# A hybrid decoder layer: SSD inputs taken from PSUM, additions moved from GpSimd, attention steps three apart

## The chip, the cores and the metric

The kernel runs on one core of one Trainium2 chip. The metric is device microseconds of one execution, the median of several. Its engines are TensorE (PE, with its weight loads as PEld), VectorE (DVE), ScalarE (ACT), GpSimd (POOL) and SyncE (SP), which issues the DMAs. Each engine works through its own queue in order; semaphores connect them.

## What is computed

One layer (DEPTH = 1) on 512 tokens of width 1024, in float32:

```python
h = rmsnorm(x, norm_mix);  u = h @ w_in          # columns: q k v | z xbc dt | p
y_attn = moba_attention(q, k, v)                  # 6 heads x 64, causal, blocks of 256
y_ssd  = ssd_mixer(xbc, z, dt_raw, ...)           # 6 heads x 64, state 128, chunks of 128
y_pool = pool_mixer(p_in, pool_w, pool_scale)     # trailing means over 2, 4, 8, 16 tokens
x = x + concat([y_attn, y_ssd, y_pool]) @ w_out
h = rmsnorm(x, norm_ffn); gate, up = split(h @ w_gate_up)
x = x + (silu(gate) * up) @ w_down                # hidden width 2816
out = rmsnorm(x, norm_final)
```

In the SSD mixer `xdt = x_h * dt`, `y = y_diag + y_off + x_h * d_skip`, then `y * silu(z)` and a norm over each group of 192 channels. With at most two blocks of 256, the block selection of the attention keeps every earlier block, so it is plain causal attention here.

## The kernel before

Products that need float32 accuracy are split: every operand becomes a rounded part and a remainder (`hi`, `lo`), and `mm3` (L165) multiplies three times, hi by hi, hi by lo, lo by hi. ACT writes the rounded part and DVE (at times POOL) subtracts it for the remainder; so each 128x1024 tile of weights costs an ACT copy and a DVE subtraction (`split`, L136).

The main line of the program writes out the projections one after the other: v, then q and k of the first two heads, the four tiles of B and C, z with dt, q and k again, the three tiles of x, q and k, and the two pooling tiles. Beside it run lanes (`Lanes`, L58): generators for attention, SSD, the transposes of x and B, and pooling. Each `mm3` advances a clock by an estimate of its time (`tick`), and a lane goes on when the clock has passed the time it asked for, or when results that it names are marked as due (`mark(name, after)` puts the due time `after` units ahead; `when` and `ensure` test it). That gives the order in which the program is written; the framework then sets the order on each engine when the kernel is built, by a simulated timeline of its own (L1245), so an engine's order need not be the written one.

The parts that the change touches:

- Attention (`attention_lane`, L635) has 24 steps, one per head and 128 queries. A step's `scores` (L585) multiplies q by k, takes the row minimum with the causal mask on DVE, the exponential and its sum on ACT, the reciprocal (L599) and the scaling of the probabilities (L600) on DVE. Two steps later (`ATT_LAG`) `probs_t` transposes the probabilities on PE (L608), and two steps after that `values` multiplies them by v. The tiles of 512 columns come from a ring of eight (`w2k`), others of 384 from a ring of six (`w384`, `NW`).
- SSD. `xs_lane` (L476) transposes a convolved tile of x on PE and ACT copies it from PSUM to `xs_nat` (L482). `ssd_decay` (L415), per chunk, builds the decay matrices; its mask addition (L424) is on DVE. POOL then makes `xdt` (L431), `xw` (L434) and `sk`, which is x times d_skip (L436). `ssd_products` (L439) does the matmuls, carries the state `prev` from chunk to chunk in two halves (L455 to L458), and sums `y`: `yo` on DVE, its addition into `sk` on POOL (L468), the diagonal part on DVE (L469), the gate `sz` on POOL (L470), the squares on ACT. After the last chunk come the norm and its scalings (L528), transposes (L533) and `mix_out`.
- Pooling. `evac_p` (L669) takes a tile out of PSUM as `pin` (L674), forms window sums by shifted additions on POOL (L677), two for the first tile and four for the second, and ends with `dm` on DVE (L691 to L693); `pool_lane` multiplies `dm` on PE (L700) and scales the product (`mix_out`, L301).
- The output projection's first half (`po`, L740) takes the eight tiles of the mixers' results in the order of `MIX_ORDER`: attention tile 0, pooling tile 0, attention 1, pooling 1, the three SSD tiles, attention 2. The second half and the FFN follow.

Of the kernel before, what the change touches and what calls it, by code (L numbers as in the profile page):

```python
# [26 lines left out]
P = 128  # L27
S = 512
# [14 lines left out]
ATT = (1.2, 0.4, 0.4)  # L43
ATT_LAG = 2
VAL_LAG = 2
SSD = (3.0, 3.0, 1.5)
LAST = 256
NDEC = 4
NW = 6
ENG = ("vvvvv", "vvvvv")  # L50
# [47 lines left out]
def layer(tc, xT, xn, w1, wz, wv, wo, wgu, wd, par, poolw, gffn, gfin, out):  # L98
# [3 lines left out]
    with ctx:  # L102
# [106 lines left out]

        warm = mp.tile([P, S], BF16, name="warm")  # L210
        nc.vector.memset(warm, 0.0)
# [132 lines left out]
        def evac_z(t, ps):  # L344
            nc.vector.scalar_tensor_tensor(dtr[:, t], ps[:, 384:390], rstd[:, t : t + 1], par_sb[:, C_DTB : C_DTB + NH], ALU.mult, ALU.add)
            th = w384(f"thz{t}")
            nc.scalar.activation(th, ps[:, :384], AF.Tanh, scale=hrstd[:, t : t + 1])
            nc.vector.tensor_scalar_mul(sz[:, t], ps[:, :384], hrstd[:, t : t + 1])
            nc.vector.scalar_tensor_tensor(sz[:, t], th, 1.0, sz[:, t], ALU.add, ALU.mult)
            if t == NT - 1:  # L350
                softplus()
                mark("dt", 13.0)

# [18 lines left out]
        bc_sb = [mp.tile([P, S], F32, name=f"bc{i}") for i in range(4)]  # L372
        xs_nat = mp.tile([P, NT, 384], F32, name="xs_nat")
        b_nat = mp.tile([P, 2, NT, P], F32, name="b_nat")
# [22 lines left out]
        ssq = mp.tile([P, 2 * NT], F32, name="ssq")  # L397
        prev = [None, None]
        skip_bc = par_sb[:, C_DSK : C_DSK + NH].unsqueeze(2).to_broadcast([P, NH, 64])
        st1 = {}  # L400
# [14 lines left out]
        def ssd_decay(c):  # L415
# [12 lines left out]
            for g in range(2):  # L428
                nc.vector.tensor_tensor(l3(es[g]), l3(es[g]), ps_g[:, None, g * P : (g + 1) * P].to_broadcast([P, 3, P]), ALU.mult)
            xdt = w384(f"xdt{c}")  # L430
            nc.gpsimd.tensor_tensor(h3(xdt), h3(xs_nat[:, c]), bcast_h(dt_, c), ALU.mult)  # L431
            xw = w384(f"xw{c}")
            if c < NT - 1:
                nc.gpsimd.tensor_tensor(h3(xw), h3(xdt), bcast_h(dte, c), ALU.mult)  # L434
            sk = w384(f"sk{c}")
            nc.gpsimd.tensor_tensor(h3(sk), h3(xs_nat[:, c]), skip_bc, ALU.mult)  # L436
            st1[c] = (es, xdt, xw, sk)

        def ssd_products(c):  # L439
            es, xdt, xw, sk = st1.pop(c)  # L440
            cs = slice(c * P, (c + 1) * P)
            if c < NT - 1:
                ps_s = bank(f"ps_s{c}")
                for g in range(2):
                    nc.tensor.matmul(ps_s[:, g * 192 : (g + 1) * 192], b_nat[:, g, c], xw[:, g * 192 : (g + 1) * 192], start=True, stop=True)
            if c > 0:
                ps_o = bank(f"ps_o{c}")
                for g in range(2):
                    nc.tensor.matmul(ps_o[:, g * 192 : (g + 1) * 192], bc_sb[2 + g][:, cs], prev[g], start=True, stop=True)
            if c < NT - 1:  # L450
                for g in range(2):
                    new = wk.tile([P, 192], F32, name=f"prev{c}{g}", tag=f"prev{g}")
                    src = ps_s[:, g * 192 : (g + 1) * 192]
                    if c == 0:
                        nc.vector.tensor_copy(new, src)  # L455
                    else:
                        nc.gpsimd.tensor_tensor(h3(new), h3(prev[g]), bcast_h(cd, c, 3, 3 * g), ALU.mult)
                        nc.vector.tensor_tensor(new, new, src, ALU.add)  # L458
                    prev[g] = new
            ps_y = bank(f"ps_y{c}")  # L460
            for h in range(NH):
                hs = slice(h * 64, (h + 1) * 64)
                nc.tensor.matmul(ps_y[:, hs], es[h // 3][:, (h % 3) * P : (h % 3 + 1) * P], xdt[:, hs], start=True, stop=True)
            L.clock += 2.6
            if c > 0:
                t_ = w384(f"yo{c}")
                nc.vector.tensor_tensor(h3(t_), h3(ps_o[:, :384]), bcast_h(ea, c), ALU.mult)
                nc.gpsimd.tensor_tensor(sk, sk, t_, ALU.add)  # L468
            nc.vector.tensor_tensor(sk, ps_y[:, :384], sk, ALU.add)  # L469
            nc.gpsimd.tensor_tensor(yz[c], sk, yz[c], ALU.mult)  # L470
            junk = w384(f"jy{c}")
            for g in range(2):
                gs = slice(g * 192, (g + 1) * 192)
                nc.scalar.activation(junk[:, gs], yz[c][:, gs], AF.Square, accum_out=ssq[:, 2 * c + g : 2 * c + g + 1])
# [18 lines left out]
        def ssd_lane():  # L493
# [20 lines left out]
            for c in range(NT):  # L514
# [6 lines left out]
                yield SSD[2]  # L521
            yield 3.0
            nc.vector.tensor_scalar(ssq, ssq, 1.0 / 192, EPS, ALU.mult, ALU.add)
            r = rsqrt(ssq, 2 * NT, "rs2")
            for c in range(NT):
                for g in range(2):
                    gs = slice(g * 192, (g + 1) * 192)
                    nc.vector.tensor_scalar_mul(yz[c][:, gs], yz[c][:, gs], r[:, 2 * c + g : 2 * c + g + 1])  # L528
            yield 7.0
            for m in range(3):  # L530
# [40 lines left out]
        def evac_k(j):  # L571
            def f(ps):
                k = w2k(f"k{j}")
                nc.vector.tensor_tensor(k, ps, rstd_bc, ALU.mult)
                for name, kl, own, other in (("ka", kl_sb[0], H0, H1), ("kb", kl_sb[1], H1, H0)):
# [93 lines left out]
        def evac_p(j):  # L669
            def f(ps):  # L670
# [581 lines left out]
```

## Time and profile before

| | |
|---|---|
| median of 3 runs (lowest to highest) | 577.88 us (576.05 to 577.88) |
| the profiled execution | 577.72 us, its span 576.0 us |
| busy in the span | PE 557.9, PEld 501.6, DVE 463.0, ACT 281.0, POOL 60.1 us |
| granted TensorE clock, mean | 0.990 |

PE busy includes its pipeline: a matmul's recorded time runs on past the start of the next. An instruction's time is from its start to its end; idle time in front of it is put down to the engine whose signal came last.

### The profile page before, as it was taken

To read this page: it belongs to the slowest core of one execution; us is meant where nothing else is said; L and a number is where in the kernel's file an instruction comes from. 1 tells how busy PE (TensorE), PEld (TensorE's weight loads), DVE (VectorE), ACT (ScalarE), POOL (GpSimd) and SP (SyncE) were. 2 spreads that over 40 slices of the span, in tenths; PEclk is the share of its full clock that TensorE was granted. 3 is DMA by queue.
4 is the path that set the end of the run, shared out by engine and by line. 5 is a ranking of instruction groups with operands and counts; after the bars stand their busy time and mean duration, and the time that the engine had idled before them with its cause. 6 is when DMAs were issued, how large, how long until landed. Compare 5 with 4: busy or idle time off the path is not lost.

```text
span 576.0 us, 9083 instructions
## 1 busy us (share of the span) xinstructions
PE 557.9 (97%) x3492; PEld 501.6 (87%) x3492; DVE 463.0 (80%) x838; ACT 281.0 (49%) x481; POOL 60.1 (10%) x75
## 2 busy tenths in 40 slices
PE   7999999999998997999999999999999999999994
PEld 4998998888776886998899989998899889899984
DVE  4387966899989768999899968897689877798445
ACT  5686554667646546464345522643155324325234
POOL 6011002006860000000000000000000000000033
PEclk8999999999999998999999999999999999999998
DMA  7862233422122701245324321443034233222003
GB/s 238 296 209 75 74 109 110 129 75 86 43 75 73 292 0 38 74 126 175 138 75 147 115 106 47 156 128 110 0 121 162 85 109 110 75 73 75 1 0 146
DMA packets 19519, 61.62 MB, mean 107 GB/s; under 512 B 2300, under 2 KB 3476, under 8 KB 19476
## 3 DMA queue, kind: packets, MB, share of 16 engines
q1 hardware_dynamic: 19476, 61.05, 31.6%
q8 instruction: 27, 0.44, 0.3%
q14 instruction: 16, 0.13, 0.1%
HBM read 58.93 MB, written 2.11 MB: 106 GB/s over the span
## 4 chain that ended last, share of the span: by engine, by line
PE 61%; DVE 7%; ACT 1%; issue 1%; DVEq 0%; ACTq 0%
PE psf L166 12%; PE psf L168 11%; PE psf L167 11%; PE pd L166 6%; PE pd L167 6%; PE pd L168 6%; PE po L166 2%; PE po L167 2%; PE po L168 2%; PE ps_h L939 1%; DVE sl L810 1%; DVE E L1059 1%; DVE x L1169 0%; DVE sz L528 0%; ACT sqf L1172 0%
## 5 line engine op out<-in xcount | busy, mean ns | idle before, releaser
L167 PE MATMUL pd<-dl,aTh 128*128 128x512 f32 x160 | 63.3, 395 | 0.0
L166 PE MATMUL pd<-dh,aTh 128*128 128x512 f32 x160 | 62.8, 396 | 0.0
L168 PE MATMUL pd<-dh,aTl 128*128 128x512 f32 x160 | 60.8, 395 | 0.0
L1059 DVE TENSOR_TENSOR E<-psf,E 128x256 f32<-128x256 f32 x110 | 42.4, 418 | 11.2 <-PE psf L168 10.3
L166 PE MATMUL psf<-h_hi,gh 128*128 128x256 f32 x176 | 49.9, 285 | 0.1
L167 PE MATMUL psf<-h_lo,sh 128*128 128x256 f32 x176 | 49.7, 282 | 0.0
L167 PE MATMUL psf<-h_lo,gh 128*128 128x256 f32 x176 | 49.7, 283 | 0.0
L168 PE MATMUL psf<-h_hi,gl 128*128 128x256 f32 x176 | 49.6, 282 | 0.0
L168 PE MATMUL psf<-h_hi,sl 128*128 128x256 f32 x176 | 49.5, 281 | 0.0
L166 PE MATMUL psf<-h_hi,sh 128*128 128x256 f32 x176 | 49.5, 281 | 0.0
L138 DVE TENSOR_TENSOR wlo<-raw,whi 128x1024 fp32r<-128x1024 f32 (+3 forms) x29 | 33.6, 1159 | 18.0 <-ACT whi L137 17.9
L1151 POOL TENSOR_TENSOR x<-x,gf 128x512 f32<-128x512 f32 x4 | 5.1, 1294 | 359.5 <-ACT sqf L774 359.5
L137 ACT ACTIVATE whi<-raw 128x1024 fp32r<-128x1024 f32 (+3 forms) x34 | 31.6, 931 | 22.0 <-PE pc L167 10.0
L166 PE MATMUL pc<-hT_hi,whi 128*128 128x512 f32 x104 | 41.3, 397 | 0.0
L809 ACT ACTIVATE sh<-sb 128x1024 fp32r<-128x1024 f32 x22 | 23.2, 1056 | 36.3 <-PE pd L167 29.8
L168 PE MATMUL pc<-hT_hi,wlo 128*128 128x512 f32 x104 | 40.9, 393 | 0.0
L167 PE MATMUL pc<-hT_lo,whi 128*128 128x512 f32 x104 | 40.8, 392 | 0.0
L766 DVE TENSOR_TENSOR x<-pd,x 128x512 f32<-128x512 f32 x44 | 28.4, 686 | 14.9 <-PE pd L168 14.8
L809 ACT ACTIVATE dh<-r_d 128x1024 fp32r<-128x1024 f32 x22 | 23.1, 1057 | 33.9 <-PE psf L167 22.6
L168 PEld LDWEIGHTS pd<-dh,aTl 128*128 128x128 f32 x160 | 30.1, 188 | 7.3
L166 PEld LDWEIGHTS pd<-dh,aTh 128*128 128x128 f32 x160 | 30.1, 188 | 7.0
L167 PEld LDWEIGHTS pd<-dl,aTh 128*128 128x128 f32 x160 | 30.1, 188 | 6.9
(291 smaller groups left out, 1714.3 us busy)
## 6 DMA issues: line engine op xcount, KB each, us to landing
r_g<-wgu SPq DMA_DIRECT2D x22, 512.0 KB, 3.7
r_u<-wgu SPq DMA_DIRECT2D x22, 512.0 KB, 3.9
r_d<-wd SPq DMA_DIRECT2D x22, 512.0 KB, 3.2
raw<-w SPq DMA_DIRECT2D x13, 512.0 KB, 3.5
raw<-wo SPq DMA_DIRECT2D x8, 512.0 KB, 3.2
rawx<-xT SPq DMA_DIRECT2D x8, 256.0 KB, 3.8
rawn<-xn SPq DMA_DIRECT2D x4, 512.0 KB, 5.1
x<-xn SPq DMA_DIRECT2D x4, 512.0 KB, 7.2
```

What stands on the lines that cost most here:

```text
L137: nc.scalar.activation(hi[:, sl], raw[:, sl], AF.Copy)
L138: eng.tensor_tensor(lo[:, sl], raw[:, sl], hi[:, sl].bitcast(F32), ALU.subtract)
L166: nc.tensor.matmul(ps, s_hi, m_hi, start=first, stop=False)
L167: nc.tensor.matmul(ps, s_hi, m_lo, start=False, stop=False)
L168: nc.tensor.matmul(ps, s_lo, m_hi, start=False, stop=last)
L766: nc.vector.tensor_tensor(x1[t][:, cs], ps, x1[t][:, cs], ALU.add)
L809: nc.scalar.activation(hi, src, AF.Copy)
L810: eng.tensor_tensor(lo, src, hi.bitcast(F32), ALU.subtract)
L939: nc.tensor.transpose(pst[:, j * P : (j + 1) * P], xh[:, kt * P : (kt + 1) * P], ident)
L1059: nc.vector.tensor_tensor(o_, a_, b_, ALU.add)
L1151: nc.gpsimd.tensor_tensor(x1[t][:, :512], x1[t][:, :512], gf[0][:, :512], ALU.mult)
```

## The change

`x*dt` and `x*d_skip` are made directly from the transposes in PSUM, for all four chunks of a tile at once: `xdt` by one DVE product, `skp` by two scaled ACT copies per tile. The lane that does it now also waits for `dt`. `xs_nat` and the per-chunk POOL products go. The additions of `yo` and the six shifted additions of pooling move from POOL to DVE. The state is one tile of 384 columns instead of two of 192; its first copy is on ACT. The probabilities of the third and fourth 128 queries of each head are scaled on ACT instead of DVE. Attention's transposes come three steps after the scores. Due times change for k (5 to 7), pooling (10 to 16) and the x tiles (1 to 2.5), the 384-column ring has three buffers, the warm-up tile lies in `xdt`'s memory, and the squares are written into `sk`.

```diff
-ATT_LAG = 2
+ATT_LAG = 3
-NW = 6
+NW = 3
+E_KL = "g"
+E_SH = "vvvvvv"
+E_YO = "v"
+E_SZ = "g"
+E_PREV = "g"
+E_PR = "vvaa"
+E_RS = "v"
+E_XW = "g"
+M_K = 7.0
+M_DM = 16.0
+M_DT = 13.0
...
+        eng = {"v": nc.vector, "g": nc.gpsimd}
...
-        warm = mp.tile([P, S], BF16, name="warm")
+        xdt = mp.tile([P, NT, 384], F32, name="xdt")
+        warm = xdt[:, 0, : S // 2].bitcast(BF16)
...
-            xdt = w384(f"xdt{c}")
-            nc.gpsimd.tensor_tensor(h3(xdt), h3(xs_nat[:, c]), bcast_h(dt_, c), ALU.mult)
-            xw = w384(f"xw{c}")
+            xw = None
             if c < NT - 1:
-                nc.gpsimd.tensor_tensor(h3(xw), h3(xdt), bcast_h(dte, c), ALU.mult)
-            sk = w384(f"sk{c}")
-            nc.gpsimd.tensor_tensor(h3(sk), h3(xs_nat[:, c]), skip_bc, ALU.mult)
-            st1[c] = (es, xdt, xw, sk)
+                xw = w384(f"xw{c}")
+                eng[E_XW].tensor_tensor(h3(xw), h3(xdt[:, c]), bcast_h(dte, c), ALU.mult)
+            st1[c] = (es, xw)
...
+            sk = skp[:, c]
...
             if c < NT - 1:
-                for g in range(2):
-                    new = wk.tile([P, 192], F32, name=f"prev{c}{g}", tag=f"prev{g}")
-                    src = ps_s[:, g * 192 : (g + 1) * 192]
-                    if c == 0:
-                        nc.vector.tensor_copy(new, src)
-                    else:
-                        nc.gpsimd.tensor_tensor(h3(new), h3(prev[g]), bcast_h(cd, c, 3, 3 * g), ALU.mult)
-                        nc.vector.tensor_tensor(new, new, src, ALU.add)
-                    prev[g] = new
+                new = wk.tile([P, 384], F32, name=f"prev{c}", tag="prev")
+                if c == 0:
+                    nc.scalar.copy(new, ps_s[:, :384])
+                else:
+                    eng[E_PREV].tensor_tensor(h3(new), h3(prev[0]), bcast_h(cd, c), ALU.mult)
+                    nc.vector.tensor_tensor(new, ps_s[:, :384], new, ALU.add)
+                prev[0] = new
...
-                nc.gpsimd.tensor_tensor(sk, sk, t_, ALU.add)
+                eng[E_YO].tensor_tensor(sk, sk, t_, ALU.add)
             nc.vector.tensor_tensor(sk, ps_y[:, :384], sk, ALU.add)
-            nc.gpsimd.tensor_tensor(yz[c], sk, yz[c], ALU.mult)
-            junk = w384(f"jy{c}")
+            eng[E_SZ].tensor_tensor(yz[c], sk, yz[c], ALU.mult)
...
         def xs_lane(m, xs):
-            yield when(f"conv{m}")
+            yield when(f"conv{m}", "dt")
...
-            nc.scalar.copy(xs_nat[:, :, m * P : (m + 1) * P], psx.rearrange("p (c n) -> p c n", c=NT))
-            mark(f"xs{m}", 1.0)
+            src = psx.rearrange("p (c h d) -> p c h d", c=NT, h=2)
+            dst = lambda t_: t_[:, :, m * P : (m + 1) * P].rearrange("p c (h d) -> p c h d", h=2)
+            dt_bc = dt_[:, :, 2 * m : 2 * m + 2].unsqueeze(3).to_broadcast([P, NT, 2, 64])
+            nc.vector.tensor_tensor(dst(xdt), src, dt_bc, ALU.mult)
+            for h in range(2):
+                c0 = C_DSK + 2 * m + h
+                nc.scalar.activation(dst(skp)[:, :, h], src[:, :, h], AF.Copy, scale=par_col(c0))
+            mark(f"xs{m}", 2.5)
...
-                mark(f"k{j}", 5.0)
+                mark(f"k{j}", M_K)
...
-            nc.vector.tensor_scalar_mul(pr[:, :n], pr[:, :n], sm)
+            if E_PR[i] == "v":
+                nc.vector.tensor_scalar_mul(pr[:, :n], pr[:, :n], sm)
+            else:
+                nc.scalar.activation(pr[:, :n], pr[:, :n], AF.Copy, scale=sm)
...
-                def shift_add(dst, src, n, p0=0):
-                    nc.gpsimd.tensor_tensor(dst[p0:, 16:], src[p0:, 16:], src[p0:, 16 - n : 16 - n + S], ALU.add)
+                def shift_add(e, dst, src, n, p0=0):
+                    eng[E_SH[e]].tensor_tensor(dst[p0:, 16:], src[p0:, 16:], src[p0:, 16 - n : 16 - n + S], ALU.add)
...
-                mark(f"dm{j}", 10.0)
+                mark(f"dm{j}", M_DM)
```

## Rows read from the trace of the kernel before

**Rows 1.** Page, busy us (share) and instructions of each engine.

```profile
PE 557.9 (97%) x3492; PEld 501.6 (87%) x3492; DVE 463.0 (80%) x838; ACT 281.0 (49%) x481; POOL 60.1 (10%) x75
```

**Rows 2.** Stretches: length; busy PE, PEld, DVE, ACT, POOL; clock, DMA, GB/s.

```profile
30.00:130.00 100.00, 100.00 (x525) 87.65 (x524) 82.39 (x181) 62.46 (x124) 7.12 (x11) 1.00 0.34 108
130.00:187.00 57.00, 53.69 (x311) 44.98 (x310) 52.55 (x122) 35.06 (x85) 32.22 (x36) 1.00 0.21 69
...
176.30:213.50 37.20, 37.05 (x180) 30.98 (x181) 28.98 (x64) 20.53 (x38) 1.30 (x1) 1.00 0.38 142
```

**Rows 3.** Waits of weight loads, 130:187: us, times, longest.

```profile
PEld po L166 <- ACT mixT_hi L301: 1.8, 1, 1.8
PEld ps_t L608 <- DVE mn L597: 1.4, 2, 1.1
PEld ps_t L608 <- DVE sk L469: 0.8, 1, 0.8
PEld po L166 <- DVE yo L467: 0.8, 1, 0.8
PEld ps_pool L700 <- DVE y L629: 0.7, 1, 0.7
```

**Rows 4.** Timeline at 154.5: start, us, engine, line [idle before <-releaser].

```profile
154.53 1.31 POOL L470 TENSOR_TENSOR sz<-sk,sz 128x384 f32<-128x384 f32 x1 [1.05 <-DVE sm L599]
...
154.90 0.97 DVE L693 TENSOR_TENSOR dm<-dm,pin 128x16 f32<-128x16 f32 x1
```

**Rows 5.** Timeline, 162 to 177 us.

```profile
162.01 0.69 DVE L674 TENSOR_TENSOR pin<-pc,rstd_bc 128x512 f32<-128x512 f32 x1
...
171.35 0.17 DVE L693 TENSOR_TENSOR dm<-dm,pin 128x16 f32<-128x16 f32 x1
171.38 1.03 POOL L468 TENSOR_TENSOR sk<-sk,yo 128x384 f32<-128x384 f32 x1 [1.88 <-DVE dm L692]
...
171.74 0.88 DVE L600 TENSOR_SCALAR pr<-pr,sm 128x384 f32<-128x384 f32 x1
...
173.42 1.05 PE L700 MATMUL ps_pool<-dm,pw 128*128 128x512 f32 x2
...
175.62 0.67 ACT L301 ACTIVATE mixT_hi<-ps_pool,par_sb 128x512 fp32r<-128x512 f32 x1
...
176.34 0.50 PE L166 MATMUL po<-whi,mixT_hi 128*128 128x512 f32 x1 [1.54 <-ACT mixT_hi L301]
```

**Rows 6.** POOL, 130:187: lines (busy, mean ns); busy us of L677.

```profile
L436 POOL TENSOR_TENSOR sk<-xs_nat,par_sb 128x384 f32<-128x384 f32 x4 | 4.8, 1195 | 0.0
...
L468 POOL TENSOR_TENSOR sk<-sk,yo 128x384 f32<-128x384 f32 x3 | 4.0, 1320 | 4.7 <-DVE yo L467 2.8 <-DVE dm L692 1.9
L431 POOL TENSOR_TENSOR xdt<-xs_nat,dt__221 128x384 f32<-128x384 f32 x4 | 3.8, 941 | 15.1 <-ACT xs_nat L482 15.1
...
130.00:187.00 57.00, 7.65 (x6) 1.00 0.21 69
```

**Rows 7.** DVE, L600: 130:187 by shape; busy us in 30:130.

```profile
L600 DVE TENSOR_SCALAR pr<-pr,sm 128x384 f32<-128x384 f32 x3 | 2.2, 742 | 0.1
...
L600 DVE TENSOR_SCALAR pr<-pr,sm 128x512 f32<-128x512 f32 x3 | 1.9, 638 | 0.0
...
30.00:130.00 100.00, 4.74 (x14) 1.00 0.34 108
```

**Rows 8.** DVE, L424: 40:130, then 130:187.

```profile
L424 DVE TENSOR_TENSOR dec<-dec,mask_s 128x384 f32<-128x384 f32 x4 | 2.0, 552 | 0.7 <-DMA dec<-acum_d 0.7
...
L424 DVE TENSOR_TENSOR dec<-dec,mask_s 128x384 f32<-128x384 f32 x4 | 3.1, 780 | 0.2 <-DMA dec<-acum_d 0.2
```

**Rows 9.** Timeline of DVE at 178 us.

```profile
178.82 1.93 DVE L528 TENSOR_SCALAR sz<-sz,rs_y 128x192 f32<-128x192 f32 x8
```

**Rows 10.** Timeline: an exponential's sum and its reciprocal.

```profile
154.68 0.19 ACT L598 ACTIVATION_READ_ACCUMULATOR pr<-pr,mn 128x1 f32 x1
...
156.63 0.16 DVE L599 RECIPROCAL sm<-sm 128x1 f32<-128x1 f32 x1
```

More of the change, by code (lines that the diff above doesn't have):

```diff
@@ L48 @@
 NDEC = 4
-NW = 6
+NW = 3
[10 more added lines that the diff above has]
+M_DT = 13.0
+D_SN = (3.0, 7.0)
 ENG = ("vvvvv", "vvvvv")
@@ L351, in evac_z @@
                 softplus()
-                mark("dt", 13.0)
+                mark("dt", M_DT)
         def softplus():
@@ L372, in layer @@
         bc_sb = [mp.tile([P, S], F32, name=f"bc{i}") for i in range(4)]
-        xs_nat = mp.tile([P, NT, 384], F32, name="xs_nat")
+        skp = mp.tile([P, NT, 384], F32, name="skp")
         b_nat = mp.tile([P, 2, NT, P], F32, name="b_nat")
@@ L397, in layer @@
         ssq = mp.tile([P, 2 * NT], F32, name="ssq")
-        prev = [None, None]
-        skip_bc = par_sb[:, C_DSK : C_DSK + NH].unsqueeze(2).to_broadcast([P, NH, 64])
+        prev = [None]
         st1 = {}
@@ L448, in ssd_products @@
                 for g in range(2):
-                    nc.tensor.matmul(ps_o[:, g * 192 : (g + 1) * 192], bc_sb[2 + g][:, cs], prev[g], start=True, stop=True)
+                    nc.tensor.matmul(ps_o[:, g * 192 : (g + 1) * 192], bc_sb[2 + g][:, cs], prev[0][:, g * 192 : (g + 1) * 192], start=True, stop=True)
             if c < NT - 1:
-                for g in range(2):
-                    new = wk.tile([P, 192], F32, name=f"prev{c}{g}", tag=f"prev{g}")
-                    src = ps_s[:, g * 192 : (g + 1) * 192]
-                    if c == 0:
-                        nc.vector.tensor_copy(new, src)
-                    else:
-                        nc.gpsimd.tensor_tensor(h3(new), h3(prev[g]), bcast_h(cd, c, 3, 3 * g), ALU.mult)
-                        nc.vector.tensor_tensor(new, new, src, ALU.add)
-                    prev[g] = new
+                new = wk.tile([P, 384], F32, name=f"prev{c}", tag="prev")
[5 more added lines that the diff above has]
+                prev[0] = new
             ps_y = bank(f"ps_y{c}")
@@ L462, in ssd_products @@
                 hs = slice(h * 64, (h + 1) * 64)
-                nc.tensor.matmul(ps_y[:, hs], es[h // 3][:, (h % 3) * P : (h % 3 + 1) * P], xdt[:, hs], start=True, stop=True)
+                nc.tensor.matmul(ps_y[:, hs], es[h // 3][:, (h % 3) * P : (h % 3 + 1) * P], xdt[:, c, hs], start=True, stop=True)
             L.clock += 2.6
@@ L521, in ssd_lane @@
                 yield SSD[2]
-            yield 3.0
+            yield D_SN[0]
             nc.vector.tensor_scalar(ssq, ssq, 1.0 / 192, EPS, ALU.mult, ALU.add)
@@ L527, in ssd_lane @@
                     gs = slice(g * 192, (g + 1) * 192)
-                    nc.vector.tensor_scalar_mul(yz[c][:, gs], yz[c][:, gs], r[:, 2 * c + g : 2 * c + g + 1])
-            yield 7.0
+                    r_ = r[:, 2 * c + g : 2 * c + g + 1]
+                    if E_RS == "v":
+                        nc.vector.tensor_scalar_mul(yz[c][:, gs], yz[c][:, gs], r_)
+                    else:
+                        nc.scalar.activation(yz[c][:, gs], yz[c][:, gs], AF.Copy, scale=r_)
+            yield D_SN[1]
             for m in range(3):
@@ L580, in f @@
                     nc.scalar.activation(t_[other], k[own], AF.Copy)
-                    nc.gpsimd.tensor_tensor(kl[own], k[own], t_[own].bitcast(F32), ALU.subtract)
-                mark(f"k{j}", 5.0)
+                    eng[E_KL].tensor_tensor(kl[own], k[own], t_[own].bitcast(F32), ALU.subtract)
+                mark(f"k{j}", M_K)
             return f
@@ L599, in scores @@
             nc.vector.reciprocal(sm, sm)
-            nc.vector.tensor_scalar_mul(pr[:, :n], pr[:, :n], sm)
+            if E_PR[i] == "v":
+                nc.vector.tensor_scalar_mul(pr[:, :n], pr[:, :n], sm)
+            else:
+                nc.scalar.activation(pr[:, :n], pr[:, :n], AF.Copy, scale=sm)
             return pr
@@ L674, in f @@
                 nc.vector.tensor_tensor(pt[:, 16:], ps, rstd_bc, ALU.mult)
-                def shift_add(dst, src, n, p0=0):
-                    nc.gpsimd.tensor_tensor(dst[p0:, 16:], src[p0:, 16:], src[p0:, 16 - n : 16 - n + S], ALU.add)
-                shift_add(wa_, pt, 1)
+                def shift_add(e, dst, src, n, p0=0):
+                    eng[E_SH[e]].tensor_tensor(dst[p0:, 16:], src[p0:, 16:], src[p0:, 16 - n : 16 - n + S], ALU.add)
+                shift_add(3 * j, wa_, pt, 1)
                 if j == 0:
-                    shift_add(wb_, wa_, 2, 64)
+                    shift_add(1, wb_, wa_, 2, 64)
                     nc.scalar.copy(wb_[:64, 16:], wa_[:64, 16:])
                 else:
-                    shift_add(wb_, wa_, 2)
-                    shift_add(wa_, wb_, 4)
-                    shift_add(wb_, wa_, 8, 64)
+                    shift_add(4, wb_, wa_, 2)
+                    shift_add(5, wa_, wb_, 4)
+                    shift_add(2, wb_, wa_, 8, 64)
                     nc.scalar.copy(wb_[:64, 16:], wa_[:64, 16:])
```

4 lines of the change are left out of this document (2 added, 2 removed).

## The prediction

> **What bounds the kernel now.** I read the page first: TensorE (PE) is busy for 557.9 of 576.0 us [rows 1], so whatever this change does on the other engines is worth only what PE waits for them. The busy times by stretch say where that is [rows 2]. From 30 to 130 us PE never stops. From 130 to 187 us, where the tail of the attention, the SSD products, the pooling and the first half of the output projection meet, it is busy for 53.7 of 57.0 us and VectorE (DVE) for 52.6: DVE is nearly full there, and PE waits for it. From 176.3 to 213.5 us PE is full again (37.1 of 37.2). Every instruction that the diff edits runs before 187 us, so the ceiling is what PE loses between 130 and 187 us: at least the 3.3 us that its busy time leaves, at most the 5.5 us that its weight loads waited at five places [rows 3]. I take about 5.
>
> The five places: 1.8 us for the second pooling tile's scaled copy on ScalarE (ACT), 1.4 and 0.8 for DVE in front of transposes of probabilities, 0.8 in front of an output projection, 0.7 for `y` in front of the first pooling matmul. I followed them back in the timeline. At 154.53 us GpSimd (POOL) starts `sz`, which ends at 155.84; a DVE subtraction of 16 columns that starts at 154.90 takes 0.97 us and ends at 155.87 [rows 4], where the same line took 0.17 us at 171.35 [rows 5]. `y` stands behind it. At 171.38 POOL adds `yo` into `sk`, and the DVE scaling at 171.74 takes 0.88 us [rows 5]; with POOL nearly idle that line's mean over all widths is 0.34 us (4.74 over 14) [rows 7]. The 1.8 us end a long chain: the second pooling tile leaves PSUM at 162.01, four additions run on POOL, DVE ends it at 171.52, PE multiplies at 173.42, and ACT delivers at 176.29, 0.05 us before PE starts [rows 5]. So POOL is in most of them, as a link of the chain or by DVE being held.
>
> **The change, part by part, for 130 to 187 us.**
>
> *POOL.* It loses `x*dt` (3.8), `x*d_skip` (4.8), the additions of `yo` (4.0) and the six shifted additions (7.65): 20.2 of its 32.2 us [rows 2, 6]. The state's decay becomes one instruction per chunk instead of two.
>
> *DVE, what comes.* Four shifted additions of 512 columns and two on part of the partitions, at the 0.69 us of a 512-column two-operand pass [rows 5]: 4.1. Three additions of `yo` at the 0.55 us of a 384-column pass in quiet [rows 8]: 1.7. Three products `x*dt` from PSUM at 0.69, of which I count one here, since two of the three convolutions end earlier, where PE has no waits: 0.7. Sum 6.5.
>
> *DVE, what goes.* The six widest probability scalings of this stretch: 2.2 + 1.9 [rows 7]. The state's first copy goes to ACT and two half-width additions become one: two passes near 0.35, 0.7. Sum 4.8.
>
> *DVE, what gets shorter.* In this stretch the mask addition takes 0.78 us against 0.55 in quiet [rows 8], the 384-wide scaling 0.74 against the 0.34 of rows 7. So the four scalings that stay could lose 0.4 each, four mask additions 0.23, the 16-column line 0.8; for the rest (splits, `qa`, `qb`, `dm`), which have no row here, I put 1.5: 4.8 if POOL were silent. With 20.2 of 32.2 gone I take 3.1. The new additions read two operands from SBUF as the mask addition does, so they meet what is left on POOL: from 9 x 0.23 x 0.37 = 0.8, if they fare as the mask additions did beside a POOL 57% busy, to 9 x 0.80 = 7.2, if each is held as the 16-column line was. I take 0.8, as the mask additions are the likest. Net for DVE: 6.5 - 4.8 - 3.1 + 0.8 = -0.6 us. DVE is hardly relieved; what goes is POOL from the chains.
>
> For this the Trainium skill, "SBUF — State Buffer", section "Who interferes with whom", has a rule: a VectorE instruction with two SBUF inputs, or in a two-port mode, and a GpSimd instruction that reads SBUF shut each other out for the whole instruction. By that rule, the trace agrees: the two ends at 155.84 and 155.87. It speaks against the change too, which puts nine such instructions where DVE is fullest; it is the mechanism of the third rival below.
>
> *The waits of PE.* First pooling matmul: 0.7 goes. Transposes behind held scalings: 0.4 and 0.5 of their 1.4 and 0.8. The projection in front of which 0.8 was waited reads the first pooling tile, whose chain shortens: 0.5. The second pooling tile: 9.5 us from PSUM to `dm` become 0.69 + 4 x 0.69 + about 1.1 = 4.6 plus queueing, so 1.6 of 1.8 goes. Sum 3.7. What is late next is the SSD tail, whose normalisation ends on DVE at 180.75 [rows 9]. If PE arrives 3.7 us sooner, that tail must follow. It loses a POOL pass of 1.03 and 0.5 of being held [rows 5], and starts about 1.2 sooner because PE's own products do: 2.7. PE then waits 1.0 us there. Gain 3.7 - 1.0 = 2.7, with a tenth for short waits elsewhere 2.8.
>
> *ScalarE.* It gets the 12 scalings, six of them here, at most 0.67 us each as in the scaled copy of 512 columns [rows 5]: 4.0 us, and six half-width scaled copies instead of three whole ones, about 1 us more. It is busy for 35.1 of 57.0 us [rows 2], which hides the work. A new wait comes: the scaling waits for DVE's reciprocal, and everything behind it on ACT (splits of weights, copies for the next projections, exponentials) waits too, and PE for those. On one step the exponential's sum was out at 154.87 and the reciprocal ran at 156.63 [rows 10]: 1.8 us. The bounds are 0 and 6 x 1.8 = 10.8 us of ACT, against 17 us idle after the additions; I take none on the path and keep the upper end as a rival.
>
> *Order.* Attention three steps apart gives each exponential one more step before PE transposes it, and keeps one more 512-column tile of a ring of eight alive; the `mark` times of the keys (5 to 7) and of pooling (10 to 16) only shift where PE's instructions are written out. Bounds: 2.9 us less (the three waits that are not a pooling tile's) to 1.8 more (one more wait as long as the longest) [rows 3]; I take nothing beside the sum above, which has part of it. The smaller ring (NW 6 to 3) goes with three fewer kinds of tile in it, and the transposes of x wait for `dt`, which is written out a projection earlier: nothing. No DMA is added, and those that SP issues keep their places.
>
> **Sum.** 577.72 us (the profiled execution: span 576.0 and 1.7 around it) - 2.8 = 574.9 us. The median of the runs shown is 577.88, practically the same. A difference under 0.3% (1.7 us) can't be told from none.
>
> **Rivals.**
>
> *The late order eats the gain.* The pooling matmul is written out at 16 clock units instead of 10; if PE's order keeps it where it was, the shorter pooling chain is not used, and of 3.7 only the 1.6 us of the held scalings and `y` go, less the 1.0 at the SSD tail: 577.1. For it: the two pooling waits are 2.1 of the 3.7. Against: the order on PE need not be the written one.
>
> *ACT stands in its own way: slower.* Place: a scaling that waits for the reciprocal, in front of the scaled copy on which PE already waited 1.8 us [rows 3]. Price: 1.8 + 0.67 = 2.5 us there, with the other gains lost: 580.2. It decides once the reciprocal is late by 1.5 us or more in DVE's queue at one of the two pooling tiles. For it: DVE stays 91% full. Against: ACT is idle for 22 of the 57 us.
>
> *Additions held by POOL.* Nine held for 0.80 us: DVE +5.8 instead of -0.6, where 4.4 us of it are idle; the 1.4 us over go to PE and no wait is saved: 579.1. Against it stand the mask additions.
>
> *More than forecast.* All 5 us of PE's loss go, the SSD tail following: 572.7.
>
> **How the numbers follow.** Forecast 0.46, late order 0.24, ACT 0.14, held additions 0.06, more 0.10. The forecast's own range is 573.3 to 576.6, and some nine tenths of it lie over 0.3%: 0.41; with the last case and the lower edge of the late order 0.54 faster. Most of the ACT case, under half of the held additions and a little of the late order are 0.17 slower; 0.29 stay within. For 8 in 10 the range takes the forecast and the late order, most of the larger gain and of the other two: 572.0 to 580.0.
>
> **What the changed profile would show.** POOL's busy time between 130 and 187 us near 12 us; no 16-column line of 0.97 us; scalings that stay on DVE near 0.35 us; from `pin` to the finished `dm` under 7 us; PE's weight loads waiting under 3 us there, most of it for the SSD tail; the stretch after 213 us unchanged, 2 to 3 us earlier. It is wrong if ACT idles before its scalings with PE waiting for a copy behind them, if a shifted addition takes over 1 us, or if the gain or loss lies after 190 us.

## The result, and the profile after

| | before | after |
|---|---|---|
| median of six runs, us | 577.88 (576.05 to 579.16) | 573.43 (570.86 to 573.94) |
| profiled execution, us (span) | 577.72 (576.0) | 570.86 (569.1) |
| mean granted clock of that execution | 0.990 | 0.996 |

The ratio of the times is 0.9917, with an interval from 0.9897 to 0.9937: 4.8 us less, 3.6 to 6.0. Forecast was 2.8 us less.

The two spans lie 6.9 us apart, and two parts of that aren't the change's. The first is the start. In the next fence and the one behind it (stretches; columns as in [rows 2]), PE's clock was granted at 0.72 on average between 6 and 12 us before, and at 1.00 after. The main line's products of the first q and k come first (from 7.1 us before, 5.9 after); the projection of v (`pn`), which follows them, begins at 20.0 us before and at 18.1 us after: 1.9 us. That early the diff touches nothing but the memory of the warm-up tile, and the runs don't show that as the reason: the other kernels with the old tile begin the projection of v at 18.3 to 19.8 us, those with the new one at 18.1 to 19.7. The second is a stretch at half clock among the first products of the FFN, which of this pair only the execution before has. It is read under "half clock" below and is worth 0.85 us. The runs of both kernels fall into groups by mean clock, and like with like (spans 571.7 to 572.2 against 575.5 to 577.5 at 0.988 to 0.991, or 569.1 and 569.2 against some 574.5 at 0.994 to 0.996) the difference is 4 to 5 us, as the ratio has it.

```profile
6.00:12.00 6.00, 4.89 (x13) 3.67 (x14) 4.05 (x4) 4.51 (x7) 3.77 (x4) 0.72 0.89 301
...
224.00:227.00 3.00, 0.36 (x2) 0.37 (x3) 3.00 (x6) 0.23 (x1) 0.00 (x0) 0.94 0.00 0
227.00:230.00 3.00, 3.00 (x16) 2.99 (x15) 1.98 (x4) 1.44 (x3) 0.00 (x0) 0.50 0.49 158
```

The kernel after, its stretches (the second answers to [rows 2]):

```profile
6.00:12.00 6.00, 5.42 (x22) 3.83 (x23) 3.82 (x4) 4.50 (x7) 4.47 (x4) 1.00 0.89 302
...
130.00:187.00 57.00, 56.16 (x325) 48.16 (x324) 52.51 (x126) 37.33 (x88) 11.13 (x16) 1.00 0.32 109
...
218.00:221.00 3.00, 0.38 (x3) 0.38 (x4) 3.00 (x6) 0.21 (x1) 0.00 (x0) 1.00 0.00 0
221.00:224.00 3.00, 2.90 (x26) 2.69 (x25) 2.80 (x6) 1.91 (x4) 0.00 (x0) 1.00 0.43 161
```

Between 130 and 187 us POOL fell from 32.22 to 11.13 us, DVE stayed where it was (52.55 and 52.51), and PE's idle time fell from 3.3 to 0.84 us. What its weight loads still wait for there (answers to [rows 3]):

```profile
PEld ps_t L630 <- ACT pr L622: 0.9, 1, 0.9
PEld po L179 <- DVE skp L478: 0.7, 1, 0.7
PEld ps_o L460 <- issue: 0.6, 1, 0.6
PEld ps_t L630 <- issue: 0.5, 2, 0.3
```

The waits for a pooling tile's copy (1.8) and for DVE ahead of transposes of probabilities (1.4 and 0.8) are gone; no new one stands at the SSD tail. First and last starts of two tiles' matmuls, before and then after (min, median and max ns, first and last start in us), show where the time was won:

```profile
L166 PE MATMUL po<-whi,mixT_hi x64: 387/389/497, 158.9 to 215.6; 128*128 128x512 f32 x64
...
L166 PE MATMUL psf<-h_hi,gh x176: 277/280/561, 219.3 to 538.3; 128*128 128x256 f32 x176
```

```profile
L179 PE MATMUL po<-whi,mixT_hi x64: 387/389/501, 151.8 to 209.6; 128*128 128x512 f32 x64
...
L179 PE MATMUL psf<-h_hi,gh x176: 277/280/385, 213.3 to 531.4; 128*128 128x256 f32 x176
```

With the 1.9 us of the start taken off, the output projection ends 4.1 us sooner, and the FFN begins 4.1 us sooner.

For every kernel below I added up what PE lost: each interval between the starts of two neighbouring matmuls, less the steady interval of their form (0.227 us for 512 columns), and what a half clock adds counts too. Three sums: "early" runs from the projection of v (`pn`) to the last projection of the mixers (`pc`), "tail" from there to the last transpose of the SSD result (`ps_sn`), "later" from there to the first down projection of the FFN. The times are the ratios against the runs of before beside them on the same chip, turned into microseconds of 577.5. "Half" counts the stretches at the lower clock level between 30 and 560 us of the profiled execution. The sums depend on the steady interval that is taken for each form; differences between kernels hold to some 0.4 us.

| kernel | ratio (95%) | us | early | tail | later | half |
|---|---|---|---|---|---|---|
| before | 1 | 0 | 2.9 | 6.2 | 7.0 | 1 |
| after | 0.9917 (0.9897-0.9937) | -4.8 | 2.4 | 2.5 | 6.1 | 0 |
| b1_adds_pool | 0.9930 (0.9911-0.9949) | -4.0 | 2.4 | 3.4 | 6.1 | 0 |
| b2_lag2 | 0.9968 (0.9954-0.9981) | -1.8 | 2.4 | 5.3 | 7.1 | 1 |
| b3_scal_dve | 0.9992 (0.9979-1.0005) | -0.5 | 3.0 | 6.2 | 7.2 | 1 |
| b5_xs_pool | 1.0031 (1.0017-1.0046) | +1.8 | 2.5 | 7.0 | 9.3 | 2 |
| b4_due | 1.0043 (1.0029-1.0058) | +2.5 | 6.1 | 5.2 | 7.2 | 1 |
| c_mk5 | 1.0031 (1.0016-1.0047) | +1.8 | 6.2 | 4.5 | 7.4 | 1 |
| c_mk9 | 0.9965 (0.9951-0.9979) | -2.0 | 3.3 | 3.6 | 7.2 | 0 |
| a1_adds | 1.0047 (1.0029-1.0064) | +2.7 | 3.4 | 7.1 | 8.9 | 1 |
| a2_lag3 | 1.0114 (1.0082-1.0146) | +6.6 | 4.8 | 12.1 | 6.3 | 2 |
| a3_xs | 0.9994 (0.9980-1.0008) | -0.3 | 5.0 | 4.7 | 6.4 | 0 |
| d_before_due | 1.0006 (0.9990-1.0022) | +0.3 | 2.5 | 6.1 | 7.2 | 1 |
| d_before_duelag3 | 0.9998 (0.9986-1.0011) | -0.1 | 2.4 | 6.6 | 7.3 | 2 |

One execution of a2_lag3 (3117 us) and one of d_before_duelag3 (1938 us) are left out of the ratios. Of the 4.95 us that the profiled pair differ by from the projection of v on, some 3.7 lie in the tail, 0.5 before it and 0.85 after it (each rounded).

### The profile page after: what moved, and what is told of

Read it like the earlier page. It is cut to its first block, busy times and chain, and to the rows that moved or that the text cites. A ratio compares the mean times of both kernels' runs of the same rounds, so it can differ in the third digit from the quotient of the medians.

```text
span 569.1 us, 9071 instructions
## 1 busy us (share of the span) xinstructions
PE 553.4 (97%) x3492; PEld 498.8 (88%) x3492; DVE 459.6 (81%) x834; ACT 288.8 (51%) x497; POOL 40.8 (7%) x56
## 4 chain that ended last, share of the span: by engine, by line
PE 85%; DVE 10%; ACT 2%; issue 1%; DMA 1%; SPq 0%; DVEq 0%; ACTq 0%
PE psf L179 12%; PE psf L181 12%; PE psf L180 12%; PE pd L180 7%; PE pd L179 7%; PE pd L181 6%; PE pc L179 4%; PE pc L180 4%; PE pc L181 4%; PE po L179 2%; PE po L180 2%; PE po L181 2%; PE pn L180 2%; PE pn L179 2%; PE pn L181 2%
## 5 line engine op out<-in xcount | busy, mean ns | idle before, releaser
L832 DVE TENSOR_TENSOR sl<-sb,sh 128x1024 fp32r<-128x1024 f32 x22 | 26.8, 1220 | 9.3 <-ACT sh L831 5.5
```

The costliest lines, as they stand in the source:

```text
L832: eng.tensor_tensor(lo, src, hi.bitcast(F32), ALU.subtract)
```

## The experiments

My theory after the result was the prediction's: POOL out of the chains of the additions, so that PE waits for them no longer. The rivals: the new order (steps three apart, and the keys' and pooling's due times), the scalings on ACT, and `x*dt` and `x*d_skip` from PSUM. The b and c kernels are the kernel after with one part undone; the a and d kernels are the kernel before with one part done (a3_xs is after with the rest undone). Every such edit also changes the order in which PE's instructions are written out, so a difference is that of the part with the order it leads to.

**b1_adds_pool: the nine additions back on POOL.**

```diff
-E_SH = "vvvvvv"
-E_YO = "v"
+E_SH = "gggggg"
+E_YO = "g"
```

> The changed kernel with the six shifted additions and the three additions of yo put back on GpSimd; all else as changed. If GpSimd in the chains was what TensorE waited for (my theory), the pooling chain is 9 to 10 us again and TensorE loses 2 to 3 us more between the projections' end and the output projection: 575.5 to 576.5, over half of the 4.5 us gone. If the third step between scores and transposes gave the gain (first rival), the additions are covered and the time stays within 1 us of the changed kernel: 573 to 574.5. If the late due time of pooling hides the chain (second rival), also no loss, and the pooling matmul stands where it stands in the changed kernel, with dm finished just before it instead of 9 us before.

Measured 0.9930, not to be told from after. Its timeline (start, us, engine, line):

```profile
151.54 0.69 DVE L696 TENSOR_TENSOR pin<-pc,rstd_bc 128x512 f32<-128x512 f32 x1
...
157.50 0.56 DVE L478 TENSOR_TENSOR skp<-ps_y,skp 128x384 f32<-128x384 f32 x1 [2.27 <-POOL skp L477]
...
158.11 0.19 PEld L179 LDWEIGHTS po<-whi,mixT_hi 128*128 128x128 f32 x1 [2.40 <-DVE skp L478]
...
162.06 0.17 DVE L715 TENSOR_TENSOR dm<-dm,pin 128x16 f32<-128x16 f32 x1
```

The second pooling chain takes 10.7 us with its additions on POOL, and 10.6 with them on DVE (next section). What the additions on POOL cost is one wait of 2.4 us, for the addition of `yo`, where after has 0.7; the tail's loss is 0.9 us more, in line with the 0.8 of the ratios, which their intervals don't separate from nothing. The theory that the additions bring the gain falls: they are worth 0.8 of 4.8 us, and by the intervals not over some 2.4.

**a1_adds: those nine additions on DVE, alone.** Both lines of the kernel before:

```diff
-                nc.gpsimd.tensor_tensor(sk, sk, t_, ALU.add)
+                nc.vector.tensor_tensor(sk, sk, t_, ALU.add)
...
-                    nc.gpsimd.tensor_tensor(dst[p0:, 16:], src[p0:, 16:], src[p0:, 16 - n : 16 - n + S], ALU.add)
+                    nc.vector.tensor_tensor(dst[p0:, 16:], src[p0:, 16:], src[p0:, 16 - n : 16 - n + S], ALU.add)
```

> The kernel before with the six shifted additions and the additions of yo on VectorE, nothing else. My theory: the waits for the second pooling tile and for y go, less what VectorE now carries: 575 to 576, 2 to 3 us under before. First rival: VectorE, already full there, takes 5.8 us more and is no faster, 577.5 to 579.

Measured 2.7 us slower. In 130 to 187 us POOL is down to 21.62 us, but DVE is at 55.04 of 57.0, and PE waits for what is late in its queue:

```profile
PEld ps_s L591 <- DVE prev L458: 1.2, 1, 1.2
PEld ps_sn L533 <- DVE sz L528: 1.0, 1, 1.0
```

The second is the wait of 1.0 us at the SSD tail that I had forecast for the whole change. It comes when DVE gets the additions and is relieved of nothing.

**b2_lag2: attention steps two apart again.**

```diff
-ATT_LAG = 3
+ATT_LAG = 2
```

> The changed kernel with attention's transposes two steps behind the scores again. My theory: the step has a small part, TensorE waits 0.5 to 1 us more for probabilities, 574 to 574.5. First rival (the step gives the gain): 575.5 to 577, with waits of transposes for DVE and ScalarE of 2 us or more in the trace, since the scalings on ScalarE now need a round trip in two steps.

Measured 0.9968: 3.0 us of the gain go, 2.8 of them in the tail. There PE waits 2.6 us in three places for a scaled copy on ACT (`mixT_hi`) and 1.2 at a transpose of probabilities.

**a2_lag3: steps three apart, alone.**

```diff
-ATT_LAG = 2
+ATT_LAG = 3
```

> The kernel before with ATT_LAG = 3, nothing else. My theory: two waits of transposes (1.4 and 0.8 us) shrink, the pooling waits stay, 576.5 to 577.5. First rival: most of the 4.5 us comes from here, 574 to 575.

Measured 6.6 us slower. Stretches of the tail:

```profile
166.00:170.00 4.00, 1.59 (x10) 1.06 (x8) 3.47 (x7) 2.87 (x6) 0.43 (x1) 1.00 0.12 17
170.00:174.00 4.00, 4.00 (x19) 3.61 (x19) 3.97 (x12) 1.47 (x4) 1.88 (x2) 0.57 0.33 120
178.00:181.00 3.00, 1.46 (x10) 1.08 (x9) 2.94 (x12) 1.74 (x5) 0.00 (x0) 0.97 0.00 0
181.00:185.00 4.00, 4.00 (x14) 3.05 (x14) 1.55 (x4) 1.40 (x3) 0.00 (x0) 0.59 0.00 0
```

Twice PE is busy for less than half of some 3 to 4 us, and both times 3.4 us at half clock follow. Two of them take up to 3.4 us of full-speed work. The waits of its weight loads from 151 to 192 us are 4.8 us for DVE, 1.3 for ACT, and several for which the profile shows no engine that was late (the longest 1.7).

**b3_scal_dve: the twelve scalings back on DVE.**

```diff
-E_PR = "vvaa"
+E_PR = "vvvv"
```

> The changed kernel with all probability scalings on VectorE again. My first theory (GpSimd out of the additions) has fallen: with the additions back on GpSimd the time was the same. New theory: the gain comes from x*dt and x*d_skip leaving GpSimd, which stood at the head of its queue for every chunk, together with the third step; then this version loses little, 573.5 to 574.5. Rival: VectorE's load decides, and the twelve scalings (about 7 us) are what relieved it; then 575.5 to 577.

Measured 0.9992: nearly all of the gain goes. From 130 to 187 us:

```profile
130.00:187.00 57.00, 53.29 (x305) 44.27 (x304) 55.42 (x132) 34.94 (x86) 12.64 (x17) 1.00 0.22 72
```

DVE is at 55.42 where after has 52.51, and PE loses 3.7 us more in the tail; of its four longest waits there three are for DVE (1.3, 1.1 and 0.7 us) and one for ACT (1.2). As I read it, DVE has room for the nine additions and the products because it gives these scalings away.

**b5_xs_pool: ACT copies the transposes of x, and POOL makes both products from SBUF, chunk by chunk.**

```diff
+        skip_bc = par_sb[:, C_DSK : C_DSK + NH].unsqueeze(2).to_broadcast([P, NH, 64])
...
+            nc.gpsimd.tensor_tensor(h3(xdt[:, c]), h3(skp[:, c]), bcast_h(dt_, c), ALU.mult)
...
+            nc.gpsimd.tensor_tensor(h3(skp[:, c]), h3(skp[:, c]), skip_bc, ALU.mult)
...
-            nc.vector.tensor_tensor(dst(xdt), src, dt_bc, ALU.mult)
-            for h in range(2):
-                c0 = C_DSK + 2 * m + h
-                nc.scalar.activation(dst(skp)[:, :, h], src[:, :, h], AF.Copy, scale=par_col(c0))
+            nc.scalar.copy(skp[:, :, m * P : (m + 1) * P], psx.rearrange("p (c n) -> p c n", c=NT))
```

> The changed kernel with x*dt and x*d_skip per chunk on GpSimd again, from an ACT copy of the transposes (the second product in place). New theory: this loses most of the gain, 576 to 578, with the SSD matmuls waiting for GpSimd. Rival (VectorE's load): VectorE is 2 us lighter and the time stays, 573 to 574.5.

Measured 1.0031: 6.6 us more than after, 4.5 of the loss in the tail and 3.1 later. Stretches:

```profile
149.00:150.00 1.00, 0.04 (x2) 0.04 (x1) 1.00 (x4) 0.43 (x1) 0.00 (x0) 1.00 0.02 5
154.00:155.00 1.00, 0.04 (x1) 0.04 (x1) 1.00 (x5) 0.99 (x5) 0.00 (x0) 1.00 0.00 0
156.00:160.00 4.00, 4.00 (x17) 3.57 (x16) 4.00 (x12) 1.34 (x2) 0.00 (x0) 0.57 0.17 71
```

PE is idle twice for about 1 us (149 and 154 us) with DVE busy throughout, and half clock follows from 156 us. That stretch is up to 1.7 us of the 4.5, and a second one, from 221 us on, up to 1.7 of the 3.1. The waits that I had expected, of SSD matmuls for GpSimd, aren't there: from 148 to 182 us the long ones are for ACT (a scaling, 1.4) and DVE (`y` and a row minimum, 1.2 each). So the products cost more than POOL's time; how they lead to these gaps isn't shown.

**a3_xs: only the products from PSUM** (with the one-tile state and the smaller ring; the order, the scalings and the additions as before).

```diff
-ATT_LAG = 3
+ATT_LAG = 2
...
-E_SH = "vvvvvv"
-E_YO = "v"
+E_SH = "gggggg"
+E_YO = "g"
...
-E_PR = "vvaa"
+E_PR = "vvvv"
...
-M_K = 7.0
-M_DM = 16.0
+M_K = 5.0
+M_DM = 10.0
...
-            mark(f"xs{m}", 2.5)
+            mark(f"xs{m}", 1.0)
```

> The changed kernel with everything back except x*dt and x*d_skip from PSUM, the state in one tile and the smaller ring: additions on GpSimd, scalings on VectorE, two steps, old due times. New theory: about half of the gain, 575 to 576.5, the other half coming with the third step. Rival: alone it is no better than the additions or the third step alone were, 578 to 581.

Measured 0.9994, as before. The tail loses 1.5 us less than before, but 2.1 more are lost early: PE stands before transposes of probabilities and is busy for 3.73 us of the five from 120 us on, where before it never stops.

**b4_due: the old due times** of the keys, the pooling and the transposes of x.

```diff
-M_K = 7.0
-M_DM = 16.0
+M_K = 5.0
+M_DM = 10.0
...
-            mark(f"xs{m}", 2.5)
+            mark(f"xs{m}", 1.0)
```

> The changed kernel with the due times of before (k 5, pooling 10, x tiles 1). New theory: within 1 us of the changed kernel, 573 to 574.5. Rival: the due times put the pooling matmul so late that its chain hides; with 10 units TensorE stands before it for 1 to 3 us and the time is 575 to 576.5.

Measured 1.0043, 7.3 us more than after: the dearest of all parts, and the one that I had priced at nothing. Its early loss is 6.1 us against 2.4. The rival's reason didn't show: with 10 units as with 16 PE comes to the second pooling tile some 7 us after it is ready (6.9 here, 6.4 in after).

**c_mk5 and c_mk9: only the keys' due time, 5 and 9 in place of 7.**

```diff
-M_K = 7.0
+M_K = 5.0
```

> The changed kernel with the due time of k at 5 instead of 7, nothing else. In every run so far with 5 the first transpose of x stands at 111 to 113 us, with 7 at 107 to 108. Theory of the order: a later k lets the x projections pass in front of the attention's second head pair, SSD starts 4 to 5 us sooner, and this is what putting the three due times back lost; then 578 to 580 and the transposes at 111 to 113 us. Rival: the pooling due time (16) or that of the x tiles did it; then 573 to 574.5.

> The changed kernel with k due at 9. Theory of the order, if later is better still: x's transposes at 105 to 106 us and 571 to 573.5. Rival: 7 lets the x projections pass already, and 9 only makes the attention's tail late: 574 to 577.

c_mk5 has 1.0031, so this one number carries nearly all of b4's loss; c_mk9 has 0.9965, 2.8 us more than after. Of the three values 7 is the best, and none of the versions run beats the kernel after. In c_mk5 the transposes of x start at 113.4 us, in after at 106.9. Waits of its weight loads between 113 and 130 us, and its timeline there:

```profile
PEld ps_t L630 <- ACT pr L622: 2.0, 1, 2.0
PEld pc L179 <- ACT skp L497: 1.6, 1, 1.6
```

```profile
114.23 1.04 ACT L150 ACTIVATE whi<-raw 128x1024 fp32r<-128x1024 f32 x1
...
115.18 0.80 ACT L398 ACTIVATE ca<-cin,halfw 128x512 f32<-128x512 f32 x1
...
115.88 0.60 ACT L622 ACTIVATE pr<-pr,sm 128x384 f32<-128x384 f32 x1
...
116.49 0.84 ACT L497 ACTIVATE skp<-ps_xn,par_sb 128x256 f32<-128x256 f32 x2
...
117.38 0.50 PE L179 MATMUL pc<-hT_hi,whi 128*128 128x512 f32 x1 [1.39 <-ACT skp L497]
```

Here the work that the change gave to ACT stands in a row behind a weight split and a convolution's product: a scaling, then the scaled copies out of the transposes' PSUM bank, and PE can't go on. These two waits of 3.6 us are nearly all of the 3.8 us of early loss that c_mk5 has over after; 2.0 more are lost in the tail and 1.3 later. With the due time at 7 the first transposes of x come at 106.93 us, their scaled copies run on ACT only at 110.11, 2.6 us after these end, and PE has other work all that time and waits for nothing.

**d_before_due and d_before_duelag3: the due times on the kernel before, without and with steps three apart.**

```diff
-            mark(f"xs{m}", 1.0)
+            mark(f"xs{m}", 2.5)
...
-                mark(f"k{j}", 5.0)
+                mark(f"k{j}", 7.0)
...
-                mark(f"dm{j}", 10.0)
+                mark(f"dm{j}", 16.0)
```

> The kernel before with the three new due times (k 7, pooling 16, x tiles 2.5), nothing else. Theory of the order: x's transposes at 107 to 108 us and most of the gain, 574 to 576. Rival (the parts need each other, and the order is only good for the work as the changed kernel divides it): no better than before or worse, 577 to 581, as the additions and the third step were alone.

d_before_duelag3 has `ATT_LAG = 3` besides.

> The kernel before with the three new due times and the third step; GpSimd, VectorE and ScalarE keep their work. Theory of the order: the third step cost 6 us alone because the attention stood in front of SSD and its last steps came late; with the due times it is 573.5 to 576. Rival (parts need each other): 577 to 583.

Both are as before (1.0006 and 0.9998): the new order by itself, on the old division of work, brings nothing, though with it the third step costs nothing either (a2_lag3 alone: 6.6). Why the tail keeps its loss, in the timeline and in stretches of d_before_duelag3:

```profile
151.10 0.93 DVE L600 TENSOR_SCALAR pr<-pr,sm 128x256 f32<-128x256 f32 x1
...
152.14 0.80 DVE L600 TENSOR_SCALAR pr<-pr,sm 128x384 f32<-128x384 f32 x1
...
153.55 0.30 PE L608 MATMUL ps_t<-ident,pr 128*128 128x128 f32 x1 [1.19 <-DVE dec L429]
```

```profile
152.00:156.00 4.00, 1.91 (x11) 1.34 (x9) 3.96 (x10) 2.75 (x9) 2.96 (x5) 1.00 0.00 0
156.00:160.00 4.00, 3.67 (x13) 3.14 (x13) 2.11 (x8) 0.62 (x1) 3.81 (x6) 0.58 0.39 131
```

Two scalings take 0.93 and 0.80 us beside POOL's `sz`, `x*dt` and `x*d_skip` (150.79 to 153.63 without a gap), PE comes to their transposes 1.2 us too soon, is busy for 1.91 of 4 us, and gets half the clock from 156.6 us on. The kernel after has neither those scalings on DVE nor those products on POOL.

## Why the prediction was right or wrong

The side and the size hold: 573.4 lies in the likeliest case's own range, at its lower edge. The way there was another one, so the number is in good part luck. By its steps:

*The bound* was right, *the ceiling* somewhat low. PE lost 6.2 us in the tail, where I had put 5.5 at most: beside the five waits of [rows 3] there are five shorter ones, 1.5 us together. 3.7 came back; outside the tail 0.5 before it and the 0.85 of the half clock.

*POOL, DVE, and the prices* were right. POOL 11.13 us (12 forecast), DVE unchanged (-0.6 forecast). The mask addition and the scalings that stayed on DVE run as in quiet (answers to [rows 7, 8]), and the 16-column line takes 0.16 to 0.18 us. One reading was too wide: 0.34 us in [rows 7] is the mean of four widths, and 384 columns alone take 0.42 in that stretch. The scalings that stayed are narrower, and lost 0.34 (256 columns, 0.74 before) and 0.40 us (128 columns, 0.68), so the 0.4 came out. The lines after:

```profile
L437 DVE TENSOR_TENSOR dec<-dec,mask_s 128x384 f32<-128x384 f32 x4 | 2.1, 550 | 1.1 <-DMA dec<-acum_d 1.0
...
L620 DVE TENSOR_SCALAR pr<-pr,sm 128x256 f32<-128x256 f32 x2 | 0.8, 398 | 0.0
...
L620 DVE TENSOR_SCALAR pr<-pr,sm 128x128 f32<-128x128 f32 x2 | 0.6, 279 | 0.0
```

*"9.5 us from PSUM to `dm` become ... 4.6 plus queueing, so 1.6 of 1.8 goes", and 0.5 for the first tile:* the step that failed, in two ways. The first is the reading of before. PE didn't wait for that chain: `dm` was done at 171.52, and PE's product started 1.9 us later, at 173.42 [rows 5], after a short wait for another result of DVE. The 1.8 us lay behind the product. The product ended at 174.47, PE had run its next transposes by 174.80, and ACT began the scaled copy only at 175.62, after squares and an exponential that stood before it in its queue:

```profile
173.15 0.44 PE L608 MATMUL ps_t<-ident,pr 128*128 128x128 f32 x2 [0.38 <-DVE sk L469]
...
174.31 0.49 PE L608 MATMUL ps_t<-ident,pr 128*128 128x128 f32 x3
...
174.92 0.71 ACT L598 ACTIVATE pr<-pr,mn 128x512 f32<-128x512 f32 x1
```

The second is the length. The timeline of the kernel after, with what else is needed below (answers to [rows 4, 5, 9]):

```profile
106.93 0.60 PE L489 MATMUL ps_xn<-ident,xs 128*128 128x128 f32 x4
...
110.11 0.82 ACT L497 ACTIVATE skp<-ps_xn,par_sb 128x256 f32<-128x256 f32 x2
...
151.65 0.68 DVE L696 TENSOR_TENSOR pin<-pc,rstd_bc 128x512 f32<-128x512 f32 x1
...
154.63 0.73 ACT L622 ACTIVATE pr<-pr,sm 128x512 f32<-128x512 f32 x1 [1.38 <-DVE sm L618]
...
156.40 1.01 POOL L479 TENSOR_TENSOR sz<-skp,sz 128x384 f32<-128x384 f32 x1 [4.38 <-DVE skp L478]
...
156.57 1.39 DVE L699 TENSOR_TENSOR pwa<-pwb 128x512 f32<-128x512 f32 x1
...
162.11 0.17 DVE L715 TENSOR_TENSOR dm<-dm,pin 128x16 f32<-128x16 f32 x1
...
168.68 1.12 PE L722 MATMUL ps_pool<-dm,pw 128*128 128x512 f32 x2
...
170.73 0.69 ACT L315 ACTIVATE mixT_hi<-ps_pool,par_sb 128x512 fp32r<-128x512 f32 x1
170.76 0.66 PE L630 MATMUL ps_t<-ident,pr 128*128 128x128 f32 x4 [0.62 <-ACT pr L622]
...
171.66 0.44 PE L179 MATMUL po<-whi,mixT_hi 128*128 128x512 f32 x1
...
172.12 1.92 DVE L545 TENSOR_SCALAR sz<-sz,rs_y 128x192 f32<-128x192 f32 x8
...
174.60 1.03 PE L552 MATMUL ps_sn<-ident,sz 128*128 128x128 f32 x8
```

From `pin` at 151.65 to the end of `dm` at 162.28 it is 10.6 us, more than before and not under 7: its four additions sum to 3.4 us, and most of the rest is DVE's queue between them, which the prediction had as an unnamed "plus queueing". The chain begins 10.4 us sooner (pin at 162.01 before, [rows 5]; 8.5 without the start's part) and PE comes to it 6.4 us after its end, to the first tile's 9.4 us after. The 1.8 us went because PE has transposes and other products in hand while ACT makes the copy (170.73 to 171.42), and takes up the projection at 171.66. That is the order of the work, as d_before_duelag3 shows: there POOL still makes the additions and the chain takes 11.4 us, yet `dm` is done 8.4 us before PE comes and the wait for the copy is gone too. In a1_adds, with the due times and steps of before and a chain of 10.6 us, it is gone as well. So it doesn't hang on the chain's length, and what I credited to a shorter chain is the work of the order in which PE and ACT come to their instructions.

The rival "The late order eats the gain" had one half right, for the chain's length wasn't used; the gain came without it.

*"Order ... I take nothing beside the sum above":* the same failure from the other side. The due time of the keys alone is worth 6.6 us within the change, the third step 3.0. Bounds of 2.9 less and 1.8 more, taken from waits in the trace of before, were too narrow, since a due time doesn't shift one wait: it sets which work PE has in hand while ACT and DVE are late. My sentence that due times only shift where instructions are written out is true, and that is just what counts.

*"PE then waits 1.0 us" at the SSD tail* didn't come: the normalisation starts 6.7 us sooner (178.82 before, [rows 9]), 4.8 without the start's part, and not 2.7, and PE's transposes at 174.60 find it done. In a1_adds that wait stands, at 1.0 us.

*ScalarE hidden:* nearly right. ACT idles 1.38 us for a reciprocal at 154.63 and PE waits for nothing behind it; once, at 170.76, PE waits 0.9 us for a scaling. The rival "ACT stands in its own way" is near: c_mk5 shows PE waiting 3.6 us for what stands in ACT's queue, but behind a weight split and a convolution's product and not behind a late reciprocal. The order is what keeps it away.

*Additions held by POOL:* one of six shifted additions took 1.39 us, beside POOL's `sz` (156.40 to 157.41); the others 0.67 to 0.69. A shifted addition over 1 us was one of my signs that the forecast is wrong. It came once, and my 0.8 us for the nine additions was near (0.7). By the Trainium skill, "SBUF — State Buffer", section "Who interferes with whom", a VectorE instruction with two SBUF inputs and a GpSimd instruction that reads SBUF shut each other out for the whole instruction. By that rule this one would run after `sz` and end at 158.09; the trace nearly agrees, with 157.96.

*The stretch after 213 us:* 2 to 3 us earlier was forecast; it is 4.1 without the start's part.

*Half clock.* The 0.85 us behind the tail in the profiled pair are not a gain of the change that I can show. In both kernels PE is idle for some 2.9 us after the FFN's first products, waiting 2.8 us for DVE's `xh`, the second half of its normalised input; before, 3.4 us at 1.2 GHz follow (0.50 in the first fence, from 226.6 us), after, it stays at 2.4 GHz. Of the edited kernels b1_adds_pool, a2_lag3, a3_xs and c_mk9 stay up there too, and b2_lag2, b3_scal_dve, b4_due, c_mk5 and both d kernels don't; in a1_adds and b5_xs_pool the clock falls at 221 us, just ahead of the FFN's first products. What decides between the two no run here shows.

*What makes up the 4.8 us.* On before, the products alone and the order with due times change nothing that can be told (0.3 and 0.1 us less), the additions cost 2.7 and the third step 6.6: no part that was tried alone gains. Undone one at a time on after, the additions cost 0.8 us, the third step 3.0, the scalings 4.3, the products 6.6, the due times 7.3; that is 22 us for a gain of 4.8. So the gain is of the set: that is shown. Why is read from the waits, and in part argued: the due times bring the work on x to where PE has other work (c_mk5), the third step gives the probabilities time (in b2_lag2 PE waits 1.2 us at one of their transposes, and 2.6 for scaled copies), and both pay only when DVE isn't made full by the rest (b3_scal_dve) and the products aren't on POOL (b5_xs_pool, d_before_duelag3). Left open: the scalings alone on the kernel before, the due times of pooling and of x apart from the keys', the one-tile state and the ring, and how much of each price is the order that a build then chooses.

## What to carry to other kernels

A part of a change can be worth nothing alone and more than the whole when undone, so price a set by undoing each part in the finished kernel and by doing each alone in the old one. Where instructions are ordered from due times, don't bound an edit of them by the waits that the old trace happens to show (here 1.8 us, against 6.6 measured): move one and measure. Before a chain is priced, compare its end with the start of its reader: if the reader comes later, it isn't waited for, and shortening it gives nothing. A chain that is no longer waited for hasn't become shorter either.

## What the runs showed of the hardware

After stretches in which PE stood idle for 1 us or more its clock fell to 0.50 for 3.4 us each time (1.7 us of full-speed work), in the tail of a2_lag3 twice, of b5_xs_pool and d_before_duelag3 once, but not after every such gap: 0.38 us busy out of 3 from 218 us on in the kernel after left it at 1.00. A gap of PE can so cost more than its length.

The four mask additions of DVE from 130 to 187 us take 0.55 us each beside 11 us of POOL (after) and 0.83 beside 23 (b1_adds_pool), so what is near POOL's work pays for it even where the whole time doesn't show it. POOL's total alone doesn't set the price: it is 0.72 beside 14 us in c_mk9, and 0.70 in a2_lag3 but 1.11 in d_before_due, both beside 32.
